# Making the values of a decoder block by seven products of quarters in place of eight

## The chip, the cores and the metric

The kernel runs on one core of one Trainium2 chip. The metric is the device time of one execution in microseconds (us); several executions are timed and their median is compared.

## The reference

The program is one decoder block on a sequence of 1024 positions with 1024 channels. What the change touches is the projection that makes the values, and, beside it, the projection whose result gates a pooling branch. All numbers are float32. Cut to what matters, the reference is:

```
h = rms_norm(x, norm_gain) * (1.0 + scale) + shift          # 1024 positions x 1024 channels
proj = h @ w_in                                             # eight blocks of 1024 columns
q, k, v, z_a, u, z_b, m_a, m_b = split(proj)
attn = stick_breaking_attention(q, k, v)                    # 16 heads of 64
p_a = (attn * silu(z_a)) @ w_branch_a
pooled = multiscale_causal_pool(u, pool_w, pool_scale)      # window means of u minus u, mapped
p_b = (pooled * silu(z_b)) @ w_branch_b
out = (sigmoid(m_a) * p_a + sigmoid(m_b) * p_b) @ w_out
return rms_norm(x + gate * out, final_gain)
```

## The kernel before, in words

Every float32 product is made as three matmuls. Each operand is split into a high part, rounded to the matmul's format by a cast on ACT, and a low part, which DVE makes as the operand minus its high part; high times high, high times low and low times high are summed in PSUM. One matmul has a stationary tile of 128x128 and a moving tile of 128x512, and so a product of a 1024x1024 matrix with another takes 8 x 8 x 2 x 3 = 384 matmuls.

The modulated input h is kept on the chip for most of the run as `hT` (line 152): channels on the partitions, eight blocks of 128 channels, 1024 positions, high and low part. It is made in two halves of 512 positions. The stages around the change follow one another on TensorE (PE):

1. **u.** The columns u of the projection, with the pooling map multiplied into the weights ahead (`mapped`, line 308; the tiles `wg` of the pool `first`). The second half of the positions is the loop at line 554; each result is copied out of PSUM by ACT and stored to `u_d` in HBM (`copy_out`, line 172).
2. **v.** The values, lines 547 to 592. Each of two halves of the 1024 value columns has four weight blocks (`load_wv`, line 548: a load of 512 KB, a cast on ACT, a subtraction on DVE). For each of 16 results of 128 positions x 512 columns there are 24 matmuls into one PSUM bank: the stationary tile is a piece of `hT`, the moving one a weight block. ACT and DVE split the result into `vo`, and SP stores that to `v_d`. Under these matmuls the pooling windows of the first channel blocks are made too: `load_u` reads a block back from `u_d`, `make_d` (line 530) adds shifted copies on DVE and leaves the difference `d`. The table `DIFFS` (line 39) says behind which results this is written for the blocks 0 to 3.
3. **wzb.** Eight blocks of z_b, line 626: `project` (line 158) loads and splits a weight block and makes two results; `silu` applies the activation on ACT and multiplies by `d` on DVE, into `gb`. DVE also forms sums of `gb`'s quarters (`t1`, `t2`) there, and one column of the gate from each block of `w_gate` (line 646; the tile `wg` of the pool `pb` has one buffer).
4. **branch b.** `gb` times `w_branch_b`, lines 652 to 738, which is already made by seven products of 512x512 quarters (a Strassen scheme in Winograd's form): the tuple `products` (line 685) lists them as p1, p5, p6, p7, p4, p3, p2 with the weights' operand a and the other operand b. Some operands are sums or differences of quarters, made on DVE. Each product has two halves q of 24 matmuls that go over four PSUM banks, six matmuls at a time; p1, p6, p7 and p4 are added up in the same four banks, p5 and p3 in four others, with copies taken in between.

The order of the instructions in these stages is not the program's. A scheduler orders each engine's instructions when the program is built, from a model of their costs; afterwards every engine runs its own list strictly in order, and so do the DMA queues of SP and ACT. PSUM has eight banks, named by the tags `pj`, `z`, `av` and `tr` with two each; `any_bank` takes the tags in turn. The weights' raw loads go through two buffers `raw`, the split weights through two buffers `whl`, both in the pool `wts`. From the attention on (line 741) most of the order is written out by hand.

Of the kernel before, what the change touches and what calls it, by code (L numbers as in the profile page):

```python
# [9 lines left out]
F32 = mybir.dt.float32  # L10
F32R = mybir.dt.float32r
# [4 lines left out]
P = 128  # L16
D = 1024
S = 1024
KB = D // P
# [19 lines left out]
DIFFS = {1: 0, 4: 1, 7: 2, 10: 3}  # L39
HD = 64  # L40
# [12 lines left out]
def block_kernel(ctx, tc, a, out):  # L53
# [17 lines left out]
    turns = cycle(("pj", "z", "av", "tr"))  # L71

    def any_bank(name):
        return bank(next(turns), name)
# [471 lines left out]

    with pool("vp") as vp:
        def load_wv(hf, k2):
            raw = wts.tile([P, 2, 512], F32, tag="raw", bufs=2, name=f"wv{hf}_{k2}_raw")
            nc.sync.dma_start(raw.rearrange("p k c -> p (k c)"), a["w_v"][hf, k2])  # L550
            return split(raw, [P, 2, 512], vp, "wv", 6, act, v, f"wv{hf}_{k2}")

        wv = [[load_wv(0, k2) for k2 in range(4)]]
# [5 lines left out]
        diffs = ExitStack()  # L559
        todo = []  # L560
        dif = diffs.enter_context(pool("dif", side="right"))
        vouts = ExitStack()
        vop = vouts.enter_context(pool("vop", side="right"))
        for hf in range(2):
            if hf == 0:
                wv.append([load_wv(1, k2) for k2 in range(4)])
            for sb in range(8):
                ss = slice(sb * P, (sb + 1) * P)
                ps = any_bank(f"v{sb}_{hf}")
                for kb in range(KB):  # L570
                    hh, hl = h_hi[:, kb, ss], h_lo[:, kb, ss]
                    wh, wl = (w[:, kb % 2] for w in wv[hf][kb // 2])
                    for n, (l, w) in enumerate(((hh, wh), (hh, wl), (hl, wh))):
                        mm(ps, l, w, start=kb == 0 and n == 0, stop=kb == KB - 1 and n == 2)

                vo = vop.tile([P, 8, 2, HD], F32R, tag="vo", bufs=3, name=f"vo{sb}_{hf}")
                pv = ps.rearrange("p (h d) -> p h d", d=HD)
                act.copy(vo[:, :, 0], pv)
                v.tensor_sub(vo[:, :, 1], pv, vo[:, :, 0].bitcast(F32))
                nc.sync.dma_start(  # L580
                    v_d[4 * hf:4 * hf + 4, :, sb].rearrange("n p c -> p n c"),
                    vo.rearrange("p (n h) i d -> p n (h i d)", h=2).bitcast(F32),
                )

                now, todo = todo, []
# [3 lines left out]
                for f in now:  # L589
                    f()  # L590
        assert not todo
        vouts.close()


# [12 lines left out]

    def b_op(src, name):
        hl = pb.tile([P, 2, 2, 512], F32R, tag="bhl", bufs=3, name=name)
        act.copy(hl[:, 0], src)  # L610
        v.tensor_sub(hl[:, 1], src, hl[:, 0].bitcast(F32))
        return hl

    def load_a(m, k, q, pl, tag, name):
        raw = pl.tile([P, 2, 512], F32, tag=tag, bufs=2, name=name)
        r0 = (4 * k + 2 * q) * P
        nc.sync.dma_start(raw, a["w_branch_b"][r0:r0 + 2 * P, 512 * m:512 * m + 512].rearrange("(k p) c -> p k c", p=P))
        return raw

    def a_op(src, name):  # L620
        hl = wts.tile([P, 2, 2, 512], F32R, tag="whl", bufs=2, name=name)
        act.copy(hl[:, 0], src)
        v.tensor_sub(hl[:, 1], src, hl[:, 0].bitcast(F32))
        return hl
# [28 lines left out]
    s2k = sums.tile([P, 4, 512], F32, name="s2k")  # L653

    def raw1(m, k, q, name):
        return load_a(m, k, q, wts, "raw", name)

    def raw2(m, k, q, name):
        return load_a(m, k, q, sums, "ar", name)

    def k2(t, q):
        return t[:, 2 * q:2 * q + 2]

    def a_s1(q):
        r, w = raw1(1, 0, q, f"a21_{q}"), raw2(1, 1, q, f"a22_{q}")
        v.tensor_add(r, r, w)
        w = raw2(0, 0, q, f"a11s_{q}")
        v.tensor_sub(k2(s2k, q), r, w)
        return r

    def a_s3(q):
        r, w = raw1(0, 0, q, f"a11d_{q}"), raw2(1, 0, q, f"a21d_{q}")
        v.tensor_sub(r, r, w)
        return r

    def a_s4(q):
        r = raw1(0, 1, q, f"a12s_{q}")
        v.tensor_sub(r, r, k2(s2k, q))
        return r

    def b_t4(q):
        v.tensor_sub(k2(t2, q), part(gb, 1, 0, q), k2(t2, q))
        return k2(t2, q)

    products = (
        ("p1", lambda q: raw1(0, 0, q, f"a11_{q}"), lambda q: part(gb, 0, 0, q)),
        ("p5", a_s1, lambda q: k2(t1, q)),
        ("p6", lambda q: k2(s2k, q), lambda q: k2(t2, q)),
        ("p7", a_s3, lambda q: part(gb, 0, 1, q)),
        ("p4", lambda q: raw1(1, 1, q, f"a22_{q}"), b_t4),  # L690
        ("p3", a_s4, lambda q: part(gb, 1, 1, q)),
        ("p2", lambda q: raw1(0, 1, q, f"a12_{q}"), lambda q: part(gb, 1, 0, q)),
    )
    ta, tb = ("pj", "pj", "z", "z"), ("av", "av", "tr", "tr")
    chain = {}
    keep = {}

    def out_b(j, n, t):
        nc.sync.dma_start(pb_d[j][:, 512 * n:512 * n + 512], t)

    def copied(tag, bufs, j, src):
        t = sums.tile([P, 512], F32, tag=tag, bufs=bufs, name=f"{tag}_{j}")
        act.copy(t, src)
        return t

    def added(t, src):
        v.tensor_add(t, src, t)
        return t

    for n, (name, a_of, b_of) in enumerate(products):  # L710
        c = {"p5": "b", "p3": "b", "p2": "c"}.get(name, "a")
        if c not in chain:
            chain[c] = [bank((tb if c == "b" else ta)[j], f"{name}_{j}") for j in range(4)]
        ps = chain[c]
        for q in range(2):
            wl_, ml_ = a_op(a_of(q), f"{name}a{q}"), b_op(b_of(q), f"{name}b{q}")
            for j in range(4):
                for e in range(2):
                    for i, (w, m) in enumerate(((0, 0), (0, 1), (1, 0))):
                        mm(  # L720
                            ps[j], wl_[:, w, e, j * P:(j + 1) * P], ml_[:, m, e],
                            start=name in ("p1", "p5", "p2") and (q, e, i) == (0, 0, 0), stop=(q, e, i) == (1, 1, 2),
                                skip_group_check=True,
                        )
# [450 lines left out]
```

## Time and profile before

| what | value |
|---|---|
| median of 3 runs | 1203.04 us (1202.47 to 1203.43) |
| the profiled execution's own time | 1203.33 us |
| its span | 1201.6 us |
| PE busy | 1189.1 us, 99% of the span |
| DVE busy | 771.5 us, 64% |
| ACT busy | 521.9 us, 43% |
| POOL busy | 255.2 us, 21% |
| mean granted TensorE clock | 0.999 of full speed |

Columns of a row of grouped instructions: the line, the engine, the operation, the output tile <- the input tiles with their shapes and the count; then the busy time and the mean ns of one; then the idle time of the engine just ahead of them and what ended it. PEld is the loading of stationary tiles, which runs beside PE. In a row of the chain of waits stand the start, the length and what ran. "SPq" and "ACTq" are DMA queues. A row of the waits reads: who waited, on whom, the total, how often, the longest.

### The profile page before, as it was taken

The page shows a single profiled execution, that of the slowest core. Times are in us where ns is not written, and L with a number is a line of the kernel's source. Part 1 is how long each engine was busy: PE and PEld are TensorE (multiplying, and loading weights), DVE is VectorE, ACT ScalarE, POOL GpSimd, SP SyncE. Part 2 cuts the span into 40 slices and gives each one's busy share as a digit, 9 for nine tenths or more (in the row PEclk, how much of TensorE's full clock was granted, in tenths as well). Part 3 has the DMA queues.
Part 4 walks back from the last instruction along what each step waited for, and adds up shares of the span by engine and source line. Part 5 has one row for each costly group of instructions (what it writes and reads, how often), then busy time and mean ns, then how long its engine had stood idle before and what let it go on. Part 6 is the DMA issues. An engine that isn't in the chain of part 4 may idle for free.

```text
span 1201.6 us, 15767 instructions
## 1 busy us (share of the span) xinstructions
PE 1189.1 (99%) x5698; PEld 993.0 (83%) x5698; DVE 771.5 (64%) x1039; ACT 521.9 (43%) x990; POOL 255.2 (21%) x384
## 2 busy tenths in 40 slices
PE   8999999999999999999999999999999999999997
PEld 7888888888888888888888888888888888888886
DVE  5752461673763486877878678786877853785643
ACT  5563121221452465555555565565655643232211
POOL 1000000000002323434334343443424431000001
PEclk9999999999999999999999999999999999999999
DMA  9634453452447432421424223242331225974612
GB/s 357 258 148 166 146 189 121 166 107 81 138 149 244 104 94 66 131 76 51 129 73 132 75 85 92 74 132 80 88 92 66 71 79 183 344 269 167 225 62 82
DMA packets 71872, 162.02 MB, mean 135 GB/s; under 512 B 9073, under 2 KB 22513, under 8 KB 69618
## 3 DMA queue, kind: packets, MB, share of 16 engines
q1 hardware_dynamic: 63586, 146.14, 38.1%
q10 hardware_dynamic: 8208, 14.88, 3.4%
q8 instruction: 45, 0.74, 0.3%
q14 instruction: 33, 0.27, 0.1%
HBM read 110.65 MB, written 33.56 MB: 120 GB/s over the span
## 4 chain that ended last, share of the span: by engine, by line
PE 91%; DVE 3%; issue 2%; DMA 2%; POOL 1%; ACT 1%; SPq 0%; POOLq 0%; ACTq 0%; DVEq 0%
PE p L102 39%; PE wzb L102 7%; PE v L102 7%; PE pa L102 7%; PE o L102 6%; PE z L102 5%; PE av L102 5%; PE wt L102 5%; PE u L102 5%; PE ua L102 3%; PE wm L102 1%; DVE om L897 1%; DMA kh<-kh 1%; DMA q<-q 0%; POOL w L117 0%
## 5 line engine op out<-in xcount | busy, mean ns | idle before, releaser
L102 PE MATMUL p<-hT,w 128*128 128x512 f32 x1920 | 479.8, 391 | 0.0
L102 PEld LDWEIGHTS p<-hT,w 128*128 128x128 f32 x1920 | 355.2, 188 | 73.9 <-DVE klo L102 0.2
L897 DVE TENSOR_TENSOR_SCAN om<-om 128x512 f32<-128x512 f32 (+7 forms) x128 | 191.3, 1494 | 87.1 <-ACT om L890 52.9
L117 POOL TENSOR_TENSOR w<-w_raw,w 128x1024 fp32r<-128x1024 f32 x39 | 97.4, 2498 | 424.5 <-ACT w L122 419.4
L890 ACT ACTIVATE om<-z 128x512 f32<-128x512 f32 (+2 forms) x192 | 94.6, 493 | 156.3 <-PE z L102 133.8
L917 DVE TENSOR_TENSOR wt<-wt,wt 128x512 fp32r<-128x512 f32 (+1 forms) x160 | 99.4, 621 | 39.5 <-ACT wt L916 38.7
L895 POOL TENSOR_SCALAR_AFFINE_SELECT om<-om 128x128 f32<-128x128 f32 x128 | 72.3, 565 | 205.3 <-ACT om L890 201.8
L916 ACT CAST wt<-wt 128x512 fp32r<-128x512 f32 (+1 forms) x160 | 88.1, 551 | 49.4 <-PE wt L102 49.0
L102 PE MATMUL av<-wt,vv 128*128 128x512 f32 x320 | 106.4, 413 | 0.0
L102 DVE TENSOR_TENSOR be<-be,om 128x511 f32<-128x511 f32 (+7 forms) x128 | 99.1, 778 | 2.0 <-POOL be L895 0.7
L891 ACT ACTIVATE be<-z 128x512 f32<-128x512 f32 (+2 forms) x192 | 94.1, 490 | 0.0
L102 PE MATMUL wt<-ident,be 128*128 128x128 f32 x576 | 89.9, 274 | 1.8 <-DVE wt L917 1.7
L102 PE MATMUL pa<-ga,wa 128*128 128x512 f32 x384 | 89.6, 389 | 0.1
L102 PE MATMUL o<-wo,mhl 128*128 128x512 f32 (+1 forms) x408 | 89.6, 377 | 0.0
L102 PE MATMUL v<-wv,hT 128*128 128x512 f32 x384 | 87.2, 389 | 0.0
L102 PE MATMUL wzb<-hT,wzb 128*128 128x512 f32 x384 | 87.2, 389 | 0.0
L102 PEld LDWEIGHTS o<-wo,mhl 128*128 128x128 f32 x408 | 73.5, 188 | 14.1
L102 PEld LDWEIGHTS pa<-ga,wa 128*128 128x128 f32 x384 | 72.0, 188 | 15.4 <-DVE wa L117 0.5
L102 PEld LDWEIGHTS v<-wv,hT 128*128 128x128 f32 x384 | 72.1, 188 | 15.0
L102 PEld LDWEIGHTS wzb<-hT,wzb 128*128 128x128 f32 x384 | 72.1, 188 | 15.0
L102 PEld LDWEIGHTS wt<-ident,be 128*128 128x128 f32 x576 | 69.8, 141 | 15.0 <-DVE wt L917 2.5
L102 PE MATMUL z<-kl,q 128*128 128x512 f32 (+2 forms) x192 | 65.5, 341 | 0.0
(172 smaller groups left out, 1378.7 us busy)
## 6 DMA issues: line engine op xcount, KB each, us to landing
w_raw<-in_w_in SPq DMA_DIRECT2D x40, 512.0 KB, 3.5
v_d<-vo SPq DMA_DIRECT2D x16, 512.0 KB, 3.1
vv<-v_d SPq DMA_DIRECT2D x8, 1024.0 KB, 5.6
wa_raw<-in_w_branch_a SPq DMA_DIRECT2D x16, 512.0 KB, 4.4
wa<-in_w_mod SPq DMA_DIRECT2D x7, 1024.0 KB, 7.0
kh<-kh SPq DMA_DIRECT2D x48, 128.0 KB, 2.3
a<-in_w_branch_b SPq DMA_DIRECT2D x10, 512.0 KB, 3.6
x<-in_x SPq DMA_DIRECT2D x8, 512.0 KB, 6.5
```

The source lines that it names most:

```text
L102: ins = op(*args, **kw)
L117: lo_eng.tensor_tensor(lo, src, hi.bitcast(F32), op=ALU.subtract)
L890: act.activation(om[:, b0:b0 + n], zp[:, :n], AF.Sigmoid, scale=-0.125)
L891: act.activation(be[:, b0:b0 + n], zp[:, :n], AF.Sigmoid, scale=0.125)
L895: gp.affine_select(out=tl[:, :P], in_=tl[:, :P], pattern=[[1, P]], compare_op=ALU.is_gt, fill=fill, base=0, channel_multiplier=-1)
L897: v.tensor_tensor_scan(om[:, :W], om[:, :W], om[:, :W], 1.0, ALU.mult, ALU.min)
L916: act.copy(wt[:, 0, :off], pt[:, :off])
L917: v.tensor_sub(wt[:, 1, :off], pt[:, :off], wt[:, 0, :off].bitcast(F32))
```

## The change

The values are made in the same way as branch b. The code of branch b becomes a function `seven`, which both use. For the values the weights are the moving operand and the input's quarters the stationary one (`a_moves`); three of the seven products (p1, p2, p3) take pieces of `hT` as they are, with their high and low parts, and four (p5, p6, p7, p4) take sums or differences of h's quarters. Those are made on DVE in the stage ahead, u, as four tiles `ht0` to `ht3` (`make_t`, one half of a tile behind each of the eight results of the loop over u), and split by ACT and DVE in front of their product (`b_op`). The weights' quarters are loaded as halves of 512 KB, 18 loads in place of 8, and added up on DVE. Of the 16 results, 12 are finished by an addition on DVE of a PSUM bank and a copy in SBUF; all are then split and stored as before (`values`). The table `DIFFS` is gone: all pooling windows are now written in the wzb stage. The loop over u takes its banks in another turn.

The core of the diff (the same code for branch b, now in `seven`, is left out):

```diff
-DIFFS = {1: 0, 4: 1, 7: 2, 10: 3}
...
-    turns = cycle(("pj", "z", "av", "tr"))
+    turns = [cycle(("av", "tr", "pj", "z")), cycle(("pj", "z", "av", "tr"))]
...
+    def b_op(src, pl, bufs, name):
+        hl = pl.tile([P, 2, 2, 512], F32R, tag="bhl", bufs=bufs, name=name)
+        act.copy(hl[:, 0], src)
+        v.tensor_sub(hl[:, 1], src, hl[:, 0].bitcast(F32))
+        return lambda m, e: hl[:, m, e]
...
+    def seven(nm, sums, load, b_of, a_moves, ta, tb, final):
+
+        s2k = sums.tile([P, 4, 512], F32, name=nm + "s2k")
+
+        def raw(first, m, k, q, name):
+            t = (wts if first else sums).tile([P, 2, 512], F32, tag="raw" if first else "ar", bufs=2, name=f"{nm}{name}_{q}")
+            load(t, m, k, q)
+            return t
+
+        def a_s1(q):
+            r, w = raw(1, 1, 0, q, "a21"), raw(0, 1, 1, q, "a22")
+            v.tensor_add(r, r, w)
+            w = raw(0, 0, 0, q, "a11s")
+            v.tensor_sub(k2(s2k, q), r, w)
+            return r
+
+        def a_s3(q):
+            r, w = raw(1, 0, 0, q, "a11d"), raw(0, 1, 0, q, "a21d")
+            v.tensor_sub(r, r, w)
+            return r
...
+        for name in ("p1", "p5", "p6", "p7", "p4", "p3", "p2"):
+            c = {"p5": "b", "p3": "b", "p2": "c"}.get(name, "a")
+            if c not in chain:
+                chain[c] = [bank((tb if c == "b" else ta)[j // 2], f"{nm}{name}_{j}") for j in range(4)]
+            ps = chain[c]
+            for q in range(2):
+                al, bl = a_op(a_of[name](q), f"{nm}{name}a{q}"), b_of(name, q)
+                for j in range(4):
+                    js = slice(j * P, j * P + P)
+                    for e in range(2):
+                        for i, (w, m) in enumerate(((0, 0), (0, 1), (1, 0))):
+                            l, r = (bl(m, e)[:, js], al[:, w, e]) if a_moves else (al[:, w, e, js], bl(m, e))
+                            mm(
+                                ps[j], l, r, start=name in ("p1", "p5", "p2") and (q, e, i) == (0, 0, 0),
+                                stop=(q, e, i) == (1, 1, 2), skip_group_check=True,
+                            )
+            for j in range(4):
+                if name == "p1":
+                    keep["s1", j] = copied("s1", 4, j, ps[j])
+                elif name == "p6":
+                    keep["s2", j] = copied("s2", 4, j, ps[j])
+                elif name == "p7":
+                    final(1, 1, j, added(copied("s3", 4, j, ps[j]), chain["b"][j]))
+                elif name == "p4":
+                    final(1, 0, j, ps[j] if a_moves else copied("s3", 4, j + 4, ps[j]))
+                elif name == "p3":
+                    final(0, 1, j, added(keep["s2", j], ps[j]))
+                elif name == "p2":
+                    final(0, 0, j, added(keep["s1", j], ps[j]))
...
     with pool("vp") as vp:
-        def load_wv(hf, k2):
-            raw = wts.tile([P, 2, 512], F32, tag="raw", bufs=2, name=f"wv{hf}_{k2}_raw")
-            nc.sync.dma_start(raw.rearrange("p k c -> p (k c)"), a["w_v"][hf, k2])
-            return split(raw, [P, 2, 512], vp, "wv", 6, act, v, f"wv{hf}_{k2}")
...
+        tq = [vp.tile([P, 4, 512], F32, name=f"ht{i}") for i in range(4)]
...
+        def difference(dst, x, y, name):
+            tmp = vp.tile([P, 2, 512], F32, tag="tmp", bufs=1, name=name)
+            v.tensor_sub(dst, x[0], y[0])
+            v.tensor_sub(tmp, x[1], y[1])
+            v.tensor_add(dst, dst, tmp)
+
+        def without(dst, x, y):
+            v.tensor_sub(dst, x[0], y)
+            v.tensor_add(dst, dst, x[1])
+
+        def make_t(i, q):
+            dst = k2(tq[i], q)
+            if i == 0:
+                difference(dst, hq(0, 1, q), hq(0, 0, q), f"tmp0_{q}")
+            elif i == 1:
+                without(dst, hq(1, 1, q), k2(tq[0], q))
+            elif i == 2:
+                difference(dst, hq(1, 1, q), hq(0, 1, q), f"tmp2_{q}")
+            else:
+                without(dst, hq(1, 0, q), k2(tq[1], q))
+
         for i in reversed(range(KB)):
             ps = any_bank(f"u{i}_1")
             mm3(ps, whl[i], h, range(KB), hmov(1))
             use[i](1, ps)
+            make_t((7 - i) // 2, (7 - i) % 2)
...
+            def values(m, n, j, src):
+                sb = 4 * n + j
+                vo = vs.tile([P, 8, 2, HD], F32R, tag="vo", bufs=3, name=f"vo{sb}_{m}")
+                pv = src.rearrange("p (h d) -> p h d", d=HD)
                 act.copy(vo[:, :, 0], pv)
                 v.tensor_sub(vo[:, :, 1], pv, vo[:, :, 0].bitcast(F32))
...
-                if 8 * hf + sb in DIFFS:
-                    j = DIFFS[8 * hf + sb]
-                    todo.append(lambda j=j, u=load_u(j): make_d(j, u))
...
+            seven("v", vs, load_v_w, h_parts, True, ("av", "tr"), ("pj", "z"), values)
```

On PE the v stage before is 16 results of four rows each (four weight blocks of six matmuls). The first two results:

```order
L102 MATMUL v0_0_1103<-wv0_0_834,hT_91 128x512 x6
L102 MATMUL v0_0_1103<-wv0_1_839,hT_91 128x512 x6
L102 MATMUL v0_0_1103<-wv0_2_844,hT_91 128x512 x6
L102 MATMUL v0_0_1103<-wv0_3_849,hT_91 128x512 x6
L102 MATMUL v1_0_1132<-wv0_0_834,hT_91 128x512 x6
```

The changed program has seven products of 48 there, 336 in all. This is the product p7: its first half q = 0 from split weights `vp7a0` and split sums `vp7b0`, and the start of the second half:

```order
L101 MATMUL vp1_0_1089<-vp7a0_1312,vp7b0_1315 128x512 x6
L101 MATMUL vp1_1_1090<-vp7a0_1312,vp7b0_1315 128x512 x6
L101 MATMUL vp1_2_1091<-vp7a0_1312,vp7b0_1315 128x512 x6
L101 MATMUL vp1_3_1092<-vp7a0_1312,vp7b0_1315 128x512 x6
L101 MATMUL vp1_0_1089<-vp7a1_1347,vp7b1_1350 128x512
L101 MATMUL vp1_1_1090<-vp7a1_1347,vp7b1_1350 128x512
L101 MATMUL vp1_2_1091<-vp7a1_1347,vp7b1_1350 128x512
L101 MATMUL vp1_3_1092<-vp7a1_1347,vp7b1_1350 128x512
L101 MATMUL vp1_0_1089<-vp7a1_1347,vp7b1_1350 128x512 x5
```

In a second half the scheduler has drawn one matmul of each bank, high part by high part, ahead of the rest, which need the low parts.

On DVE under the v stage there stood, before, pooling windows (`win`, `d`, `tl`) with a split of a result (`vo`) now and then:

```order
L536 TENSOR_TENSOR win0_1_1193<-u0_1161 128x1039
L579 TENSOR_TENSOR vo0_0_1128<-v0_0_1103,vo0_0_1128 128x8x64
L540 SCALAR_TENSOR_TENSOR d0_1195<-win0_1_1193,u0_1161 128x1023
L542 TENSOR_TENSOR tl0_1197<-win0_1_1193,invn_812 128x1
L536 TENSOR_TENSOR win1_1_1290<-u1_1258 128x1039
```

In the changed program the operands' sums and splits stand there. This is the place from the additions that finish p7 (`vs3`) to the split operands of p4's second half (`vp4a1`, `vp4b1`):

```order
L562 TENSOR_TENSOR vs3_0_1377<-vp5_0_1159,vs3_0_1377 128x512
L562 TENSOR_TENSOR vs3_1_1384<-vp5_1_1160,vs3_1_1384 128x512
L562 TENSOR_TENSOR vs3_2_1391<-vp5_2_1161,vs3_2_1391 128x512
L588 TENSOR_TENSOR va12s_0_1485<-va12s_0_1485,vs2k_1088 128x1024
L684 TENSOR_TENSOR vo4_1_1380<-vs3_0_1377,vo4_1_1380 128x8x64
L684 TENSOR_TENSOR vo5_1_1387<-vs3_1_1384,vo5_1_1387 128x8x64
L562 TENSOR_TENSOR vs3_3_1398<-vp5_3_1162,vs3_3_1398 128x512
L549 TENSOR_TENSOR vp4a1_1439<-va22_1_1437,vp4a1_1439 128x1024
L555 TENSOR_TENSOR vp4b1_1442<-ht3_835,vp4b1_1442 128x1024
```

Between p7's end and p4's second half DVE so has a weight difference for p3, two splits of results and an addition in front of the two splits that the matmuls read.

On DVE at the start of the wzb stage there stood, before, the gate columns (`wg`) and the products of the first block with a difference `d0` made long ahead:

```order
L646 SCALAR_TENSOR_TENSOR wg0_1685,gate_1619<-wg0_1685,sg_1622 128x1024
L633 SCALAR_TENSOR_TENSOR gb_1616<-d0_1195,vecs_88,gb_1616 128x512
L646 SCALAR_TENSOR_TENSOR wg1_1748,gate_1619<-wg1_1748,sg_1622 128x1024
L633 SCALAR_TENSOR_TENSOR gb_1616<-d0_1195,vecs_88,gb_1616 128x512
L637 TENSOR_TENSOR t1_1617<-gb_1616 128x512
```

In the changed program the windows start only there, and the split of the weights `wzb2` stands among them:

```order
L535 TENSOR_TENSOR win0_1_1665<-u0_1662 128x1039
L116 TENSOR_TENSOR wzb2_1824<-wzb2_raw_1822,wzb2_1824 128x1024
L539 SCALAR_TENSOR_TENSOR d0_1667<-win0_1_1665,u0_1662 128x1023
L541 TENSOR_TENSOR tl0_1669<-win0_1_1665,invn_812 128x1
L729 SCALAR_TENSOR_TENSOR wg0_1734,gate_1658<-wg0_1734,sg_1661 128x1024
L716 SCALAR_TENSOR_TENSOR gb_1655<-d0_1667,vecs_88,gb_1655 128x512
```

What moved: the reading back of u and all windows from under the v stage to under the wzb stage, where the multiplications by `d` now follow them directly.

More of the change, by code (lines that the diff above doesn't have):

```diff
@@ L544, in make_d, with a_op @@
         dhls[j] = d
[L547 to L553 removed]
+    def a_op(src, name):
+        hl = wts.tile([P, 2, 2, 512], F32R, tag="whl", bufs=2, name=name)
+        act.copy(hl[:, 0], src)
+        v.tensor_sub(hl[:, 1], src, hl[:, 0].bitcast(F32))
+        return hl
@@ new lines, in b_op, with k2, added, a_s4 @@
+    def b_op(src, pl, bufs, name):
+        hl = pl.tile([P, 2, 2, 512], F32R, tag="bhl", bufs=bufs, name=name)
+        act.copy(hl[:, 0], src)
+        v.tensor_sub(hl[:, 1], src, hl[:, 0].bitcast(F32))
+        return lambda m, e: hl[:, m, e]
+    def k2(t, q):
+        return t[:, 2 * q:2 * q + 2]
+    def added(t, src):
+        v.tensor_add(t, src, t)
+        return t
[4 more added lines that the diff above has]
+            load(t, m, k, q)
+            return t
+        def a_s1(q):
[8 more added lines that the diff above has]
+            return r
+        def a_s4(q):
+            r = raw(1, 0, 1, q, "a12s")
+            v.tensor_sub(r, r, k2(s2k, q))
+            return r
+        a_of = dict(
+            p1=lambda q: raw(1, 0, 0, q, "a11"), p5=a_s1, p6=lambda q: k2(s2k, q), p7=a_s3,
+            p4=lambda q: raw(1, 1, 1, q, "a22"), p3=a_s4, p2=lambda q: raw(1, 0, 1, q, "a12"),
+        )
+        def copied(tag, bufs, j, src):
+            t = sums.tile([P, 512], F32, tag=tag, bufs=bufs, name=f"{nm}{tag}_{j}")
+            act.copy(t, src)
+            return t
+        chain, keep = {}, {}
+        for name in ("p1", "p5", "p6", "p7", "p4", "p3", "p2"):
[13 more added lines that the diff above has]
+                                stop=(q, e, i) == (1, 1, 2), skip_group_check=True,
+                            )
+            for j in range(4):
[11 more added lines that the diff above has]
+                    final(0, 0, j, added(keep["s1", j], ps[j]))
@@ L557, in block_kernel, with load_v_w, h_parts @@
             use[i](1, ps)
+            make_t((7 - i) // 2, (7 - i) % 2)
         early.close()
[L559 to L577, printed above, removed]
+        with pool("vs", side="right") as vs:
+            def load_v_w(t, m, k, q):
+                nc.sync.dma_start(t.rearrange("p k c -> p (k c)"), a["w_v"][m, 2 * k + q])
+            def h_parts(name, q):
+                if name in ("p1", "p2", "p3"):
+                    k, n = dict(p1=(0, 0), p2=(1, 0), p3=(1, 1))[name]
+                    return lambda m, e: hT[:, m, 4 * k + 2 * q + e, 512 * n:512 * n + 512]
+                return b_op(k2(tq[("p5", "p6", "p7", "p4").index(name)], q), vs, 2, f"v{name}b{q}")
+            def values(m, n, j, src):
+                sb = 4 * n + j
+                vo = vs.tile([P, 8, 2, HD], F32R, tag="vo", bufs=3, name=f"vo{sb}_{m}")
+                pv = src.rearrange("p (h d) -> p h d", d=HD)
                 act.copy(vo[:, :, 0], pv)
@@ L606, in part @@
         return src[:, 4 * k + 2 * q:4 * k + 2 * q + 2, 512 * n:512 * n + 512]
[L608 to L624, printed above, removed]
     for j in range(KB):
@@ L652, in block_kernel @@
     sums = pbs.enter_context(pool("sums", side="right"))
[L653 to L724, printed above, removed]
-        for j in range(4):
-            if name == "p1":
-                keep["s1", j] = copied("s1", 4, j, ps[j])
-            elif name == "p6":
-                keep["s2", j] = copied("s2", 4, j, ps[j])
-            elif name == "p7":
-                out_b(j + 4, 1, added(copied("s3", 4, j, ps[j]), chain["b"][j]))
-            elif name == "p4":
-                out_b(j + 4, 0, copied("s3", 4, j + 4, ps[j]))
-            elif name == "p3":
-                out_b(j, 1, added(keep["s2", j], ps[j]))
-            elif name == "p2":
-                out_b(j, 0, added(keep["s1", j], ps[j]))
@@ L738, in block_kernel, with branch @@
+    def branch(m, n, j, t):
+        nc.sync.dma_start(pb_d[4 * m + j][:, 512 * n:512 * n + 512], t)
+    seven("b", sums, load_b_w, g_parts, False, ("pj", "z"), ("av", "tr"), branch)
     pbs.close()
```

27 lines of the change are left out of this document (20 added, 7 removed).

## The prediction

> **What bounds the kernel now.** I read the page's busy times first, then the chain of waits over the stages around the change, then the busy time of each engine by stage.
>
> ```profile
> PE 1189.1 (99%) x5698; PEld 993.0 (83%) x5698; DVE 771.5 (64%) x1039; ACT 521.9 (43%) x990; POOL 255.2 (21%) x384
> PE 91%; DVE 3%; issue 2%; DMA 2%; POOL 1%; ACT 1%; SPq 0%; POOLq 0%; ACTq 0%; DVEq 0%
> ```
>
> PE is busy all the time, and 91% of the chain that ends last is PE. The share is an average, so the chain of waits from 60 to 400 us tells what holds in these stages:
>
> ```profile
> 80.07 48.07 PE u L102 x212
> 128.14 87.04 PE v L102 x384
> 215.18 87.04 PE wzb L102 x384
> 302.22 82.43 PE p L102 x360
> ```
>
> From 80 to 384 us the chain is nothing but matmuls that follow one another. Whatever is taken off PE here comes off the end, as long as no other engine becomes late. The stages by busy time (the end of u; v; wzb; branch b; the columns are PE, PEld, DVE, ACT, POOL, granted clock, DMA share, GB/s):
>
> ```profile
> 103.00:128.00 25.00, 25.00 (x112) 20.67 (x112) 1.91 (x4) 3.88 (x6) 0.00 (x0) 1.00 0.34 118
> 128.00:215.00 87.00, 87.00 (x385) 72.05 (x384) 37.37 (x53) 13.53 (x20) 0.00 (x0) 1.00 0.51 164
> 215.00:302.00 87.00, 87.00 (x385) 72.05 (x384) 50.92 (x69) 21.52 (x28) 0.00 (x0) 1.00 0.43 118
> 302.00:379.00 77.00, 77.00 (x338) 63.14 (x338) 49.23 (x48) 34.59 (x42) 2.41 (x1) 1.00 0.44 148
> ```
>
> The last row is the model for this change: branch b is already made by seven products, with DVE busy 49.23 of 77.00 us, and PE has no gap in it.
>
> **The matmuls removed.** A matmul of the v stage follows the one before after 87.04 / 384 = 226.7 ns. The row of branch b has 336 matmuls and 24 of the next projection; at 226.7 ns those 24 are 5.44 us, so the 336 took 82.43 - 5.44 = 76.99 us, or 229.1 ns each. Seven products on the chip thus have a slightly longer step than a plain chain. In the changed stage three products (144 matmuls) have pieces of `hT` as stationary tile, as the v stage now has: 144 x 226.7 = 32.64 us. Four (192) have split sums on both sides, as branch b has: 192 x 229.1 = 43.99 us. Together 76.6 against 87.0 us: 10.4 us less. With all at 226.7 it would be 10.9 less, with all at 229.1, 10.1.
>
> The Trainium skill, TensorE: Matmul & The Clock Gate, section Back-to-back issue gap, gives about 131 ns per matmul of 512 columns for a sustained stream of load and matmul pairs; by that figure the 48 removed matmuls would be worth 6.3 us, an estimate. The trace disagrees: its step is 226.7 ns.
>
> **The sums of h's quarters, in the u stage.** `make_t` issues 20 operations of 128x1024 on DVE. Such an addition costs 1.226 us, and a split of 128x1024 on ACT 1.052 (branch b's own groups; then, in order of time, what DVE and ACT do around the end of u):
>
> ```profile
> L668 DVE TENSOR_TENSOR s2k<-a,a11s 128x1024 f32<-128x1024 f32 x2 | 2.5, 1226 | 0.1
> L622 ACT CAST p4a<-a 128x1024 fp32r<-128x1024 f32 x2 | 2.1, 1052 | 3.0 <-PE p L102 3.0
> L117 DVE TENSOR_TENSOR wv<-wv_raw,wv 128x1024 fp32r<-128x1024 f32 x8 | 9.7, 1224 | 12.7 <-ACT wv L122 12.6
> 88.84 0.75 DVE L516 SCALAR_TENSOR_TENSOR hT<-hf,mods,hT 128x512 fp32r<-128x512 f32 x1 [1.51 <-ACT hT L515]
> 128.18 0.59 ACT L175 COPY u_sg<-u 128x512 f32<-128x512 f32 x1 [4.85 <-PE u L102]
> 134.24 1.24 DVE L536 TENSOR_TENSOR win<-u 128x1039 f32<-128x1039 f32 x1 [25.93 <-DMA u<-u_d]
> ```
>
> That is 24.5 us. DVE finishes h at 89.6 and then has only splits of `wv` (1.224 each) before it sits idle for 25.93 us until 134.24; those go away. So the sums run from about 91 to 115 us, under matmuls of u that wait for none of them, 13 us ahead of their first reader. Cost: nothing; without that cover it would be up to 24.5. Two weight splits of p1 now stand among the steps that make h's second half and delay it by 1 to 2 us; the matmuls that read these blocks stand 4 us or more further down PE's list. The new turn of the banks gives p1 those of u7, u3, u6 and u2, whose copies are long past. Nothing again.
>
> **The operands inside the v stage.** On DVE: 12 weight splits (p1's two are done before), 8 splits of sums and 8 sums of weights, 28 x 1.23 = 34.3 us; 12 additions at 0.689 and 16 splits of results at 0.687, 19.3 us. With the two wzb splits, 2.5, it is 56 us in a stage of 76.6. ACT has 20 casts and 28 copies, 21 + 16.5 = 37.5 us; branch b runs with 34.59. The groups and loads of branch b and of the v stage that these figures, and the waits below, come from (a load's last figure is the us to its landing):
>
> ```profile
> L707 DVE TENSOR_TENSOR s<-p,s 128x512 f32<-128x512 f32 x11 | 7.4, 689 | 6.6 <-PE p L102 6.1 <-ACT s L703 0.4
> L579 DVE TENSOR_TENSOR vo<-v,vo 128x512 fp32r<-128x512 f32 x15 | 10.3, 687 | 31.9 <-ACT vo L578 31.9
> L703 ACT COPY s<-p 128x512 f32<-128x512 f32 x16 | 9.4, 587 | 6.9 <-PE p L102 6.9
> L673 DVE TENSOR_TENSOR a11d<-a11d,a21d 128x1024 f32<-128x1024 f32 x2 | 2.4, 1224 | 1.8 <-DMA a11d<-in_w_branch_b 1.8
> a<-in_w_branch_b SPq DMA_DIRECT2D x6, 512.0 KB, 4.9
> x<-in_x SPq DMA_DIRECT2D x8, 512.0 KB, 6.5
> ```
>
> The sum fits; what counts is the order. I followed the list by hand, with these durations, at three places.
>
> - *p5.* ACT splits p5's sums only behind the last copy of u (about 128.8). DVE then has two splits, the sum of weights and `s2k` (about 134.6); ACT's cast of the weights stands behind a copy of p1's first bank, free after 30 of p1's matmuls, 135; the low part is there at 137.8, and p5 starts at 139.0.
> - *p6.* On DVE two weight differences for p7 stand in front of p6's splits. The second one's load is issued when p5's second split has freed its buffer, 3.1 us into p5. At 4.9 us a load it lands at 8.0, and with two more operations the low part is there at 10.4; p6 needs it four matmuls after p5's 11.0, at 11.9. Room: 1.5 us.
> - *p4.* From p7's end, DVE has the third addition done at 0.3, then 1.23 + 0.69 + 0.69 + 0.69 + 1.23 + 1.23, the low parts at 6.0. p4's second half starts at 5.5 and needs them four matmuls later, 6.4. Room: 0.4 us.
>
> SP's loads of p3's and p2's weights now stand behind stores of values, which wait for DVE's splits; by the same hand reckoning each such split is past before the load's buffer is free. I take zero for the stage's waits; the rival below has the other end.
>
> **The windows, moved under wzb.** This is what went out of the v stage:
>
> ```profile
> L536 DVE TENSOR_TENSOR win<-u 128x1039 f32<-128x1039 f32 x7 | 8.7, 1239 | 28.6 <-DMA u<-u_d 28.6
> L536 DVE TENSOR_TENSOR win<-win 128x1037 f32<-128x1037 f32 (+1 forms) x6 | 7.4, 1234 | 0.1
> L540 DVE SCALAR_TENSOR_TENSOR d<-win,u 128x1023 f32<-128x1023 f32 (+2 forms) x5 | 6.1, 1221 | 0.1
> wg<-in_w_gate SPq DMA_DIRECT2D x8, 512.0 KB, 3.5
> u<-u_d SPq DMA_DIRECT2D x8, 512.0 KB, 4.0
> DVE wg L646 <- DMA wg<-in_w_gate: 4.4, 4, 2.2
> ```
>
> With 2.1 us of small pieces it is 24.3 us; wzb's DVE time goes from 50.92 to 75.2, and with the additions and splits that finish p2 after the stage's start (3.4) to 78.6 of 87.0. DVE also waits: about 4.3 us for the first `u`, whose load now stands in SP's list behind the last value store, and about 3.2 for `wzb2`, whose cast follows the second activation. That makes 86.1. About 6 us of this stands behind the last split that PE needs at the stage's end, p1a of branch b, so I find that split done some 4 us early, and each `wzb` split between 3 and 5 us early. Behind DVE's waits stand just those splits, so the room is real but it is all there is. I take zero, with an end in the second rival.
>
> **The sum.** u 0, v -10.4, wzb 0, branch b and everything after only shifted: nothing there waits for a fixed time. The span becomes 1201.6 - 10.4 = 1191.2; 1.73 us lie around it, so the profiled execution's 1203.33 becomes 1192.9. The median of the runs is 0.29 lower, so I predict 1192.6.
>
> **Rivals.**
> *The seven products wait for their operands.* For it: DVE waited 1.8 us for a weight load in branch b, and the rooms of 1.5 and 0.4 us are small. Against it: PE waited for nothing there. If loads land after 6.5 us, as those of x did, in place of 4.9, each of p5, p6 and p4 comes about 1 us late: 3 us, 1195.6.
> *DVE bounds the end of wzb.* For it: 86 of 87 us. If the waits for `w_gate` (4.4 us in all now) come on top, twice as long, since `u` loads now stand between them, that is 8 us against some 4 of room: 4 us late, 1196.6. A stage border is also where the rule of the same page of the Trainium skill would bite (section Why this matters for your kernels: over some 3 us idle, the clock halves); with a halved clock for one window of 3.4 us it would add 1.7 us, an estimate. No stage here shows a granted clock under 1.00.
> *Slower: DVE and SP in lockstep.* `wg` has one buffer, so the next load of `w_gate` is issued only when DVE has used the last, and loads of `u` stand behind it in SP's list; if DVE arrives each time before its load, each of the eight blocks pays 3.5 us: 28.0 less 4 of room, 24 us of PE's time, 1192.6 + 24 = 1216.6. It outweighs the gain from about 2.1 us a block (10.4 + 2.4 + 4, over eight). Against it: five to eight DVE operations, 6 us or more, stand between one `wg` and the next, longer than the load.
> That the change removes fewer matmuls than it says is excluded: PE's list has 336.
>
> **How the numbers follow.** Forecast 0.70, late operands 0.13, a late wzb 0.10, lockstep 0.04; 0.03 is left for waits that just eat the gain. Within 0.2%, 2.4 us, a measurement can't tell a change from none. Faster: 0.70 + 0.13 + 0.10 = 0.93; same 0.03; slower 0.04. The range's low end is 10.9 us below the lowest run, 1202.47: 1191.6. Its high end takes in both mild rivals: 1196.6.
>
> **What would show it.** In the chain of waits, v with 336 matmuls in 76 to 77 us, wzb 87.0, no piece but PE up to branch b; DVE about 24 us busier in u, 56 in v, 75 to 79 in wzb. A wait of PE on a split (`vp6`, `vp4`, a `wzb`, branch b's first) would show a rival and its size. A v stage at 80 us or more, or a gap at branch b's start, would make the prediction wrong.

## The result, and the profile after

The changed kernel takes 1192.37 us (median of 4 runs, 1191.8 to 1194.0) where the kernel before takes 1203.24 (4 runs, 1202.47 to 1204.38): a ratio of 0.9911, 95% interval 0.9894 to 0.9928. The prediction was 1192.6, with a range of 1191.6 to 1196.6. The profiled execution of the changed kernel has an own time of 1194.0 and a span of 1192.3 us.

The page's busy times, and its line on the chain that ends last:

```profile
PE 1179.2 (99%) x5650; PEld 984.6 (83%) x5650; DVE 826.6 (69%) x1093; ACT 542.3 (45%) x1016; POOL 255.1 (21%) x384
PE 82%; DVE 7%; DMA 5%; issue 4%; POOL 1%; ACT 1%; SPq 1%; POOLq 0%; ACTq 0%; DVEq 0%
```

PE has 48 matmuls fewer, and DVE is 55 us busier. PE's share of the chain fell from 91% to 82%. The chain of waits from 60 to 400 us shows where something else came in:

```profile
80.42 48.06 PE u L101 x212
128.48 74.36 PE vp L101 x328
204.19 3.92 DMA v_d<-vo
...
271.10 12.42 DMA u<-u_d
...
314.43 1.15 DVE bp6a L549
315.62 53.39 PE bp L101 x232
```

Through u and v it is PE alone. From the end of v to p6 of branch b it runs through stores, loads of `u` and DVE's work, and only there does PE wait for it. PE's timeline says how long. The length of a row counts the last matmul in full; from one start to the next it is 0.16 us less, and so the times of stages and products are taken here. Of the kernel after (`vp` is the v stage, `bp` branch b), then of the kernel before:

```profile
128.32 11.04 PE L101 MATMUL vp<-vp1a,hT 128*128 128x512 f32 x48
139.20 11.04 PE L101 MATMUL vp<-vp5a,vp5b 128*128 128x512 f32 x48
204.48 87.20 PE L101 MATMUL wzb<-hT,wzb 128*128 128x512 f32 x384
291.52 11.17 PE L101 MATMUL bp<-p1b,bp1a 128*128 128x512 f32 x48
313.51 11.55 PE L101 MATMUL bp<-p6b,bp6a 128*128 128x512 f32 x48
324.90 11.15 PE L101 MATMUL bp<-p7b,bp7a 128*128 128x512 f32 x48
368.85 16.51 PE L101 MATMUL p<-hT,w 128*128 128x512 f32 x72
```

```profile
127.98 87.20 PE L102 MATMUL v<-wv,hT 128*128 128x512 f32 x384
215.02 87.20 PE L102 MATMUL wzb<-hT,wzb 128*128 128x512 f32 x384
302.06 11.17 PE L102 MATMUL p<-p1b,p1a 128*128 128x512 f32 x48
378.98 6.33 PE L102 MATMUL p<-hT,w 128*128 128x512 f32 x27
```

The v stage went from 215.02 - 127.98 = 87.04 to 204.48 - 128.32 = 76.16 us: 10.88 less, which is 48 matmuls of 226.7 ns to the last hundredth. wzb took 87.04 both times. Branch b took 77.33 where it took 76.92; p6 alone is 11.39 and not 10.99, a wait of 0.40. Ahead of v this execution is 0.34 later and behind branch b 0.83 longer, in work that the change does not touch (0.6 of it is a wait for a DMA at the start of the attention, which differs from one execution to the next). Together -10.88 + 0.41 + 0.34 + 0.83 = -9.30, the difference of the two spans. The medians differ by -10.87, as much as the v stage alone; with an interval of some 2 us to either side they can neither confirm nor exclude the 0.41 of branch b.

Busy time by stage, with the columns of the prediction (end of u; v; wzb):

```profile
91.00:115.00 24.00, 24.00 (x108) 19.88 (x107) 22.78 (x20) 2.95 (x5) 0.00 (x0) 1.00 0.29 101
128.00:205.00 77.00, 77.00 (x342) 63.77 (x341) 49.85 (x54) 36.55 (x49) 0.00 (x0) 1.00 0.57 187
205.00:292.00 87.00, 87.00 (x386) 72.04 (x385) 71.66 (x105) 23.03 (x31) 0.00 (x0) 1.00 0.54 174
```

All twenty sums of h's quarters stand in the first row, from 91 to 115 us. In wzb DVE is busy for 71.66 of 87 us. DVE's timeline at the places that the prediction followed by hand, and in wzb:

```profile
136.89 1.23 DVE L549 TENSOR_TENSOR vp5a<-va,vp5a 128x1024 fp32r<-128x1024 f32 x1 [1.48 <-ACT vp5a L548]
148.48 1.22 DVE L555 TENSOR_TENSOR vp6b<-ht,vp6b 128x1024 fp32r<-128x1024 f32 x1
176.59 1.22 DVE L555 TENSOR_TENSOR vp4b<-ht,vp4b 128x1024 fp32r<-128x1024 f32 x1
216.71 1.24 DVE L535 TENSOR_TENSOR win<-u 128x1039 f32<-128x1039 f32 x1 [7.11 <-DMA u<-u_d]
283.55 1.24 DVE L535 TENSOR_TENSOR win<-u 128x1039 f32<-128x1039 f32 x1 [4.70 <-DMA u<-u_d]
288.40 1.22 DVE L549 TENSOR_TENSOR bp1a<-ba,bp1a 128x1024 fp32r<-128x1024 f32 x1
```

The two waits are for the first and the last `u`. What stands ahead of the last one in SP's list, and then the times of the loads of `u` to their landing (shortest, median, longest):

```profile
270.37 0.38 SPq L732 DMA_DIRECT2D g_d<-gate  x1
271.10 0.34 SPq L526 DMA_DIRECT2D u<-u_d  x1
```

```profile
DMA to landing us min/median/max: 3.3/5.2/12.4
```

The store of the gate writes 1024 numbers of four bytes each to a place of its own. The load of `u7`, issued 0.7 us behind it, takes 12.4 us. In the kernel before the same store is issued at 261.43, and the load of weights 1.1 us behind it takes 11.9.

### The profile page after: what moved, and what is told of

It is laid out like the page before. It is cut to its first block, busy times and chain, and to the rows that moved or that the text cites. A ratio compares the mean times of both kernels' runs of the same rounds, so it can differ in the third digit from the quotient of the medians.

```text
span 1192.3 us, 15804 instructions
## 1 busy us (share of the span) xinstructions
PE 1179.2 (99%) x5650; PEld 984.6 (83%) x5650; DVE 826.6 (69%) x1093; ACT 542.3 (45%) x1016; POOL 255.1 (21%) x384
## 4 chain that ended last, share of the span: by engine, by line
PE 82%; DVE 7%; DMA 5%; issue 4%; POOL 1%; ACT 1%; SPq 1%; POOLq 0%; ACTq 0%; DVEq 0%
PE p L101 33%; PE pa L101 7%; PE o L101 6%; PE vp L101 6%; PE z L101 5%; PE av L101 5%; PE wt L101 5%; PE u L101 5%; PE bp L101 4%; PE ua L101 3%; DMA u<-u_d 2%; PE wm L101 1%; DVE om L914 1%; DMA kh<-kh 1%; DVE gb L716 1%
## 5 line engine op out<-in xcount | busy, mean ns | idle before, releaser
L101 PE MATMUL z<-kh,q 128*128 128x512 f32 (+2 forms) x192 | 64.0, 334 | 1.1 <-DMA q<-qlo 1.1
L101 PE MATMUL u<-hT,wg 128*128 128x512 f32 x240 | 55.5, 391 | 0.0
```

Of the source, the lines that this page charges most:

```text
L101: ins = op(*args, **kw)
```

## The experiments

Eleven kernels ran. Those that ran together have these medians of the kernel before beside them: the first four 1203.35, the next four 1202.74, the last three 1202.61.

**1. All but the matmuls.** The kernel before, with the sums in the u stage (written to two tiles, in turn, that no product reads) and all windows under wzb:

```diff
-DIFFS = {1: 0, 4: 1, 7: 2, 10: 3}
+DIFFS = {}
...
             use[i](1, ps)
+            make_t((7 - i) // 2, (7 - i) % 2)
...
         vouts.close()
+    diffs = ExitStack()
+    dif = diffs.enter_context(pool("dif", side="right"))
```

> This is the kernel before, eight products in the v stage, with the rest of the change put in: the twenty sums of h's quarters in the u stage (made, but read by nothing) and all window work of the eight blocks in the wzb stage. Theory (the gain is the 48 matmuls and nothing else; the DVE work it brings lies under matmuls): v 87.04 us and wzb 87.04 us as before, the median within 0.6 us of the 1203.24 of before, with at most the wait of 0.4 us in branch b's p6 that the changed kernel shows. Rival 1 (the moved work costs, and the seven products gain more than their matmuls): 1204.5 or more, with a wait of PE at the start of branch b or in its p5 and p6. Rival 2 (moving the window work out of the v stage is itself a gain): 1202 or less.

Measured: 1204.48 us (median of ten executions, nine of them from 1204.17 to 1207.61 and one of 2435.97), ratio 1.0014 (1.0004 to 1.0023). PE's timeline:

```profile
127.73 87.20 PE L102 MATMUL v<-wv,hT 128*128 128x512 f32 x384
214.77 76.78 PE L102 MATMUL wzb<-hT,wzb 128*128 128x512 f32 x338
292.21 10.74 PE L102 MATMUL wzb<-hT,wzb 128*128 128x512 f32 x46 [0.66 <-DVE wzb L117]
```

Without the matmuls nothing is gained: rival 2 is out. The sums cost nothing (v 87.04). The windows under wzb cost 1.0 us, in wzb itself (292.21 - 214.77 + 10.58 = 88.02), where the last weight split comes late; in this kernel's chain of waits a load of `u`, issued 0.7 us behind the store of the gate, stands with 12.34 us ahead of it. The median is 1.1 us above the kernel before, more than the 0.6 that the theory allowed and at the edge of rival 1, whose wait, however, was to be in branch b. So the theory holds for the gain, and its "nothing" for the windows is short by up to 1 us.

**2 and 5. The longer step of branch b.** The prediction read 229.1 ns a matmul from branch b (228.9 by the starts above) and laid it to sums split on both sides. But in the v stage the four products of such sums run at 226.7 (139.20 less 128.32 is 10.88 for p1, and p5 to p4 take the same). What differs is where the tiles lie. In the list of addresses of the compiled program, `hT`, all weight tiles and the v stage's split sums begin at 224 within 256 bytes, branch b's moving tiles at 32. Two kernels move them:

```diff
+    pb.tile([P, 16], F32, name="pad")     # 2: 64 bytes; in 5: [P, 48], 192 bytes
     sg = pb.tile([P, D], F32, name="sg")
```

> The changed kernel with 64 bytes left free in the pool of branch b, so that its split tiles begin at the same place within 128 bytes (96) as all other operands of long runs of matmuls; now they begin at 32. Theory A (the longer step of branch b, 228.9 ns against 226.7 in the v stage with the same split sums on both sides, comes from where its moving tile lies): the step falls to 226.7 ns, branch b takes 0.75 us less, so the span is 0.75 shorter, and the wait of 0.40 us in p6 stays. Theory B (as the prediction had it: a product of sums split on both sides has a longer step): the step stays at 228.9 ns. Theory C (the moving side matters, not the place: in the v stage the weights move, here the split of g): it stays at 228.9 as well.

> The changed kernel with 192 bytes left free in the pool of branch b. The tiles with which the v and wzb stages work (226.7 ns a matmul) all begin at 224 within 256 bytes; branch b's moving tiles begin at 32 (228.9 ns) and, with 64 bytes left free, at 96 (233.3 ns); with 192 they begin at 224. Theory (the moving tile's place within 256 bytes sets the step): 226.7 ns, and branch b without its wait takes 76.16 us, 0.75 less than 76.92. Rival (any move makes it worse, since the place as it was is the best one): over 228.9 ns again.

Branch b's p6 with 64 bytes, then with 192:

```profile
313.42 11.36 PE L101 MATMUL bp<-p6b,bp6a 128*128 128x512 f32 x48
```

```profile
313.04 11.04 PE L101 MATMUL bp<-p6b,bp6a 128*128 128x512 f32 x48
```

11.20 / 48 = 233.3 ns, then 10.88 / 48 = 226.7, and the other six products as p6. The first run went against all three theories as they were put: the place counts, but 64 bytes made it worse. The second came out as its theory said: branch b takes 76.16 us and has the v stage's step. That p6 has no wait in these two, with the same lists and the same 12 us for the last `u`, says how thin it is: DVE reached that `u` 77.6 us after wzb's start in run 5 (281.86), and 79.1 in the profile after.

**3. The store of the gate on another queue.**

```diff
-    nc.sync.dma_start(g_d[0].rearrange("(k p) -> p k", p=P), gate)
+    act.dma_start(g_d[0].rearrange("(k p) -> p k", p=P), gate)
```

> The changed kernel with the store of the gate vector (1024 packets of 4 bytes) issued by ACT in place of SP; in SP's list it stands one place ahead of the load of the eighth u, which lands 12.4 us after its issue where the others take 5.2. Theory A (the load is held by the small packets ahead of it in the same queue): it lands 4 to 6 us after its issue, DVE's wait of 4.7 us for it goes, and with it the wait of 0.40 us of PE in branch b's p6, so branch b takes 76.93 us in place of 77.33. Theory B (the load is slow because of the other loads beside it): it still takes over 10 us, and the 0.40 us stay. Either way the time changes by less than a measurement can tell.

DVE's two longest waits from 214 to 304 us, and the issues of the last load of `u` and of the store:

```profile
DVE win L535 <- DMA u<-u_d: 8.4, 1, 8.4
DVE gb L716 <- ACT gb L715: 4.2, 2, 3.3
```

```profile
269.14 0.33 SPq L526 DMA_DIRECT2D u<-u_d  x1
269.41 0.38 ACTq L732 DMA_DIRECT2D g_d<-gate  x1
```

DVE no longer waits for the last `u`, which lands after 3.3 us (the wait left is for the first one), p6 takes 10.99, and DVE now stands still for 4.2 us because it is ahead of PE. That is what theory A expected; theory B's over 10 us did not come. But the reason that theory A gives, the common queue, is not shown. The edit changed the order as well: the store is now issued 0.3 us behind the load and not 0.7 us ahead of it. And the next load of SP's queue, weights of branch b issued at 272.14, 2.7 us behind the store on the other queue, took 11.5 us to its landing. Run 11 tries the store on ACT's queue ahead of the load. Nor is p6 a witness: its wait is missing in runs 2 and 5 too, where the store stayed. The one execution took 1191.44 us.

**4. The sums twice.**

```diff
             make_t((7 - i) // 2, (7 - i) % 2)
+            make_t((7 - i) // 2, (7 - i) % 2)
```

> The changed kernel with each of the twenty sums of h's quarters made twice. Theory (the sums end at 113.8 us and have some 17 us of room, since p5's first split of a sum runs at 130.6): the second set takes 20 x 1.14 = 22.8 us, DVE is through with them at 136.6; behind them stand two splits, an addition, a subtraction and p5's weight split, 5.9 us, so the last of p5's first operands is there at 142.5 and not at 138.1. PE needs it about 1.2 us into p5, at 140.4: p5 begins 2.1 us late, the others follow in time, and the time is 2 us longer (1 to 4): about 1194.5. Rival 1 (the sums are on the path already): 22.8 us longer, 1215. Rival 2 (there is more room, since p5 is late by less than its operands): within 0.5 us of 1192.4.

Measured: 1195.7 us, ratio 0.9937 (0.9922 to 0.9952), 3.3 above the changed kernel. PE's two waits, and the pieces of the chain ahead of the second:

```profile
140.87 11.17 PE L101 MATMUL vp<-vp5a,vp5b 128*128 128x512 f32 x48 [1.62 <-ACT vp5a L548]
154.28 10.31 PE L101 MATMUL vp<-vp6a,vp6b 128*128 128x512 f32 x44 [1.33 <-DVE vp6b L555]
```

```profile
147.12 4.63 DMA va11d<-in_w_v
151.87 1.23 DVE va11d L583
153.09 1.15 DVE vp6b L555
```

22.8 us more on DVE cost 3.3: both rivals are out. p5 began 1.8 us late (2.1 expected; v begins at 128.21, and p1 takes 10.88). The other 1.7 are p6, by the very chain that the prediction named: the load for p7, released by p5's split, stands on DVE ahead of p6's split.

**6 and 9. The first windows back under v.** The windows' buffers are reserved beside the v stage's, and two loads of `u` are free of the value stores:

```diff
-        with pool("vs", side="right") as vs:
+        diffs = ExitStack()
+        dif = diffs.enter_context(pool("dif", side="right"))
+        first_u = []
+        with pool("vs", side="right") as vs:
...
+                if (m, n, j) == (1, 0, 3):
+                    first_u.extend(load_u(i) for i in range(2))
...
-            make_d(j, load_u(j))
+            make_d(j, first_u[j] if j < 2 else load_u(j))
```

> The changed kernel with its move of the window work undone for the first blocks: the buffers of the windows are reserved beside those of the v stage (with three buffers of differences in place of five), and the loads of u0 and u1 no longer stand behind the last store of values. The list then has the windows of the first blocks on DVE among the operands of p5, p6 and p7. Theory (what counts on DVE in the v stage is the order and not the sum): p5's first weight split stands behind the first window, whose load cannot land before 138, so it is there at 140.4, just in time; four more window operations ahead of p5's second weight split bring that to some 148 where PE needs it at 145.9, so p5 waits 1 to 3 us; the wzb stage has no wait at all, and branch b's p6 is not late: 1193 to 1195. Rival (DVE is free for 20 of the v stage's 76 us, and 13 us of windows fit): no wait in v, the 0.40 us of p6 are won, 1192.0.

> The kernel with u0 and u1 loaded ahead, with 128 bytes more left free, so that the v stage's split sums of h begin at 224 within 256 bytes again; in the run before they had come to 96, and the four products with a stationary tile there took 11.15 us each and not 10.88. Theory (that run's 1.66 us in the v stage were 1.1 of place and 0.6 of waiting for p5's second operands): p7 and p4 take 10.88 again, the v stage 76.7 to 76.9 us, wzb 87.04 and branch b 76.92 without a wait, the time 1192.3 to 1192.8. Rival (the place does not matter for the stationary side; the longer step came from DVE's windows beside it): p7 and p4 still take 11.1 us or more.

Run 6: 1193.8 us, ratio 0.9925 (0.9909 to 0.9941); run 9, one execution: 1193.06. p4 in run 6, then in run 9:

```profile
173.07 11.31 PE L101 MATMUL vp<-vp4a,vp4b 128*128 128x512 f32 x48
```

```profile
172.67 11.04 PE L101 MATMUL vp<-vp4a,vp4b 128*128 128x512 f32 x48
```

In run 6 the v stage took 77.82 us, in run 9 76.78. Theory: the missing 1.04 were the place of the split sums, here the stationary tiles. 0.62 us are left, with a wait for p5's second operands behind DVE's windows (less than the 1 to 3 expected). For that, DVE waited 19.9 us in wzb for ACT's activations in run 9, so it was ahead all the time, and branch b had no wait. So the first windows cost 0.6 us under v; under wzb, in the changed kernel, all eight cost 0 to 0.4. Run 9's one time is 0.3 above the range expected for it.

**7 and 11. Eight more additions under wzb**, in 11 with the store on ACT's queue as well:

```diff
+        sg2 = dif.tile([P, D], F32, tag="sg2", bufs=1, name=f"extra{j}")
...
         v.scalar_tensor_tensor(wg, wg, 1.0, sg, ALU.mult, ALU.mult, accum_out=gate[:, j:j + 1])
+        v.tensor_add(sg2, sg, sg)
```

> The changed kernel with one more addition of 128x1024 on DVE in each of the eight blocks of the wzb stage (it writes a tile that nobody reads). Theory (from the first load of u on, DVE and the loads that it releases are as late as PE's needs allow: the wait of 0.40 us in branch b's p6 says that no room is left): eight more operations of 1.14 us are 9.1 us, of which DVE's wait of 2.3 us for w_gate can take some, so PE waits 6 to 9 us at the end of wzb and the start of branch b, and the time is 1198 to 1201. Rival (DVE is idle for 15 us of this stage, room for all of them): 1192.4 to 1193.

> The eight further additions in the wzb stage once more, with the store of the gate vector on ACT's queue. Theory (the load of the last u behind that store took the room): with the store away, branch b's first split was there at 283.8, 8 us ahead of its need, so 9.1 us more leave PE late by some 1 us, and the clock is not halved: 1191.4 + 1 = 1192.4, at most 1194. Rival (DVE's work alone fills the stage): as without it, PE is late by 6 us, the clock halves behind that, 1199 to 1201.

One execution each: 1200.41 and 1200.53 us. p5 of branch b in run 7; the busy time around that (in the columns of the prediction); and in run 11 the issues of the store and of the last load of `u`, and DVE's wait for that load:

```profile
308.28 13.73 PE L101 MATMUL bp<-p5b,bp5a 128*128 128x512 f32 x48 [5.92 <-ACT bp5a L548]
```

```profile
302.00:308.00 6.00, 0.36 (x2) 0.00 (x0) 5.75 (x6) 3.81 (x6) 0.00 (x0) 0.90 0.00 0
308.00:312.00 4.00, 3.72 (x9) 2.96 (x10) 2.71 (x3) 0.23 (x1) 0.00 (x0) 0.50 0.81 255
```

```profile
276.15 0.38 ACTq L734 DMA_DIRECT2D g_d<-gate  x1
280.44 0.33 SPq L526 DMA_DIRECT2D u<-u_d  x1
289.08 1.24 DVE L535 TENSOR_TENSOR win<-u 128x1039 f32<-128x1039 f32 x1 [0.78 <-DMA u<-u_d]
```

Run 7 bears out its theory: 5.9 us of waiting, and behind it p5 takes 13.56 us and not 10.99, with a granted clock of 0.50 (in run 11 13.31). In run 11 the theory failed, in two ways. First, the other queue did not free the load: with the store 4.3 us ahead of it on ACT's queue it took 8.6 us to its landing, and 9.1 in run 7 with the store as far ahead on SP's. So what helped in run 3 was that the load went first. Second, DVE came to the load so late that it waited only 0.8 us for it (0.6 in run 7), and PE was as late as in run 7. With 9.1 us more the stage is thus filled by DVE's own work; the store's part is those 0.8 us at most. Run 3 says why: there DVE stands still for some 4 us, so that no 8 are free.

**10. `hT` and the weights 64 bytes up.**

```diff
-    const.tile([P, 24], F32, name="skip")
+    const.tile([P, 40], F32, name="skip")
```

> The changed kernel with 64 more bytes left free at the start of its memory, so that h and all weight tiles begin at 32 within 256 bytes and not at 224; the tiles of the v stage's split sums and of the attention stay at 224, branch b's split tiles come to 96. Theory (the place within 256 bytes counts by itself, for the moving tile above all): the step of v, wzb and the last stages goes from 226.7 to about 229 ns, branch b to 233; over some 2000 to 4000 matmuls that is 5 to 10 us, 1197 to 1203, as much as the change had won. Rival (it is the distance of the two tiles from one another that counts): v's products with h and wzb keep 226.7 ns, as both sides move together.

```profile
139.38 11.15 PE L101 MATMUL vp<-vp5a,vp5b 128*128 128x512 f32 x48
205.09 87.20 PE L101 MATMUL wzb<-hT,wzb 128*128 128x512 f32 x384
314.12 11.15 PE L101 MATMUL bp<-p6b,bp6a 128*128 128x512 f32 x48
```

One execution: 1197.39 us, 5.0 above the median of the changed kernel and 3.4 above its profiled execution; 0.4 of it is in the v stage, and 3.1 behind branch b. It is in the expected range, but by another law: wzb, whose two tiles moved together, keeps 226.7 ns, the v stage's p5 (the weights moved, the split sums not) is at 10.99 / 48 = 228.9, and branch b, at 96, has 228.9 and not the 233 of run 2. The rival fits: what counts is the distance between moving and stationary tile, within 256 bytes.

**8. Both mends.** The store on ACT's queue (run 3; here too it is issued behind the last load of `u`, by 0.8 us) and 192 bytes (run 5).

> The changed kernel with the store of the gate vector on ACT's queue and with branch b's split tiles 192 bytes up. Theory: the 0.40 us of p6 and 0.75 us of step in branch b are won, branch b takes 76.16 us, and the median is 1.1 us under that of the changed kernel, about 1191.2. If the place of the tiles does not matter, 0.4 us: 1192.0.

Measured: 1191.23 us (1190.75 to 1192.76), ratio 0.9902 (0.9885 to 0.992). All products of branch b take 10.88 us, together 76.16:

```profile
291.23 11.04 PE L101 MATMUL bp<-p1b,bp1a 128*128 128x512 f32 x48
```

Of the versions with four executions it has the lowest median, 1.1 us below the changed kernel as expected; the two intervals overlap, so that only the profile tells them apart. Run 5, with the store as it was, has the same 76.16 in branch b and 1191.08 us in its one execution: no time here shows a gain by the moved store that is clear of the spread.

## Why the prediction was right

*The matmuls.* The mechanism held (run 1: without fewer matmuls no gain), and this term was mis-sized: -10.4 forecast, -10.88 measured. The step that failed is "four have split sums on both sides, as branch b has: 192 x 229.1". What sets the longer step is the distance of the tiles (runs 2, 5, 6, 10), and in the v stage it is zero; "with all at 226.7 it would be 10.9 less" was the end of the range that came true.

*The sums of h's quarters.* Right: 91 to 115 us, under u, at no cost (v is 87.04 in run 1). That the cover has an end is run 4: a second set costs 3.3 us.

*The operands inside the v stage.* The hand-followed list was right to 0.3 us. p5's low part was forecast for 137.8, p6's for 10.4 us into p5 (149.6), p4's for 6.0 us after p7's end (177.8); by the rows above they were through at 138.1, 149.7 and 177.8. PE waited for none. DVE's busy time was 50 and not 56 us, and 72 in wzb where 75 to 79 were forecast: operations of 1.22 us that follow one another start 1.13 apart (p4's last two splits at 175.46 and 176.59). At p4 the last hundredths are luck. The closer steps were made up by a wait for a load that the list did not have:

```profile
172.51 1.23 DVE L588 TENSOR_TENSOR va12s<-va12s,vs2k 128x1024 f32<-128x1024 f32 x1 [0.29 <-DMA va12s<-in_w_v]
```


*The windows under wzb.* Here "I take zero" was the weakest step, by 0 to 0.4 us in the changed kernel and 1.0 in run 1. Of the waits that the prediction listed, the first load of `u` was 7.1 and not 4.3, and `wzb2`'s cast none; the 4.7 us for the last `u` it did not have at all, because it read SP's list for loads and not for the store of the gate between them. The trace of before had shown it: the load behind that store took 11.9 us, with nobody waiting. The low part of p1 was there at 289.6 us, 1.9 ahead of branch b's start, but that of p6 came late, so "no piece but PE" did not come true in the chain.

*The sum.* 1192.6 against 1192.37: the v stage gave 0.5 us more, and the median of before is 0.2 higher in these runs than in the three that the forecast started from. That these two alone make up the difference is luck: the interval is some 2 us to either side, and p6's 0.4 is not among them.

*The rivals.* Late operands in v: none here; run 4 shows two of the three places that it named, p5 with 1.8 us and p6 with 1.7. Its price of 3 us does not follow from its own rooms: loads 1.6 us later, against rooms of 1.5 and 0.4, would make p6 0.1 us late and p4 1.2. DVE as the bound of wzb: real, but at 0.4 us and not 4; run 7 shows it in full. It also tries the rule of the Trainium skill (TensorE: Matmul & The Clock Gate, section Why this matters for your kernels) that PE idle for over some 3 us loses half its clock. The trace agrees: after 5.9 us of waiting the granted clock is 0.50 and p5 loses 2.6 us (2.3 in run 11), where the prediction had estimated 1.7; in run 4, with waits of 1.6 and 1.3 us, it stays at 1.00. No run here has a wait between these, so the 3 us themselves are not tried. Lockstep of DVE and SP: DVE waited once for `w_gate`, 2.3 us.

What stays open: why the start of the attention waits between 0 and 1.4 us for a DMA in different executions, and how the store of the gate delays loads of the other queue too. Neither was tried.

## What to carry to other kernels

Price removed matmuls by the step of their own stage, and ask what the step depends on before carrying it over from another. Work moved to an idle engine is free only as long as each operand keeps its place in the list: count the waits ahead of it, those behind a store of many small packets too, and not the busy time. A run that moves an instruction to another queue may change its order as well: look when each was issued before you name the cause. Where a stage is full to within a few microseconds, say what the first microsecond beyond costs: here about one, and past an idle of some microseconds the half clock on top.

## What the runs showed of the hardware that I had not expected

- *Distance of the tiles.* A matmul of 128x512 with both tiles at the same place within 256 bytes follows the last in 226.7 ns; at a distance of 64 bytes it takes 228.9 (branch b; run 10), at 128 bytes 233.3 (run 2) and 232.3 (run 6). No other distances were tried. Shifting one part of the tiles by 64 bytes (run 10, one execution) cost 3 to 5 us, up to half of what the change brought.
- *A store of 1024 packets of four bytes* delays loads of 512 KB that are issued soon behind it. On the same queue they took 12.0 to 12.8 us to landing when 0.7 us behind it (the changed kernel and runs 1, 2, 4, 5, 10) and 9.1 when 4.3 behind (run 7); on the other queue 11.5 when 2.7 behind (run 3) and 8.6 when 4.3 behind (run 11). In each case that is 12.7 to 14.2 us after the store was issued. A load issued 0.3 or 0.8 us ahead of it landed after 3.3 and 3.4 (runs 3, 8).
- *The half clock* after 5.9 us of waiting: 2.6 and 2.3 us (runs 7, 11); after 1.6 the granted clock stayed at 1.00 (run 4).
